# Layer 0 of a two-layer decoder trunk: every middle tile's second product pair by blocks, with weight sums made by transfers

## The chip, the cores and the metric

The kernel runs on one core of one Trainium2 chip. The metric is device time in microseconds (us) of one launch. A core has five engines that work side by side, each from its own queue in order: TensorE (PE; its weight loads are listed apart as PEld), VectorE (DVE), ScalarE (ACT), GpSimd (POOL) and SyncE (SP), which here issues transfers. Transfers run on 16 DMA engines. Engines wait for each other by semaphores.

## The reference

One inference step of a trunk of two layers over 576 tokens: 512 of a prompt and 64 of eight samples. All data is float32, the model width is 1024 and the width of each branch 2048. Layer 0 is a gated short convolution, layer 1 an mLSTM block with four heads. What concerns layer 0:

```python
def short_conv_mixer(h, buf, w_in, conv_w, w_out):
    b_gate, c_gate, xa, z = jnp.split(h @ w_in, 4, axis=-1)
    u = c_gate * xa
    conv, new_buf = causal_dwconv(u, buf, conv_w)
    y = b_gate * conv * jax.nn.silu(z)
    return y @ w_out, new_buf
```

Here `h` is the RMS-normalised input (576 x 1024) and `w_in` is 1024 x 8192. Layer 1 projects to 2 x 2048, convolves, makes queries, keys and values (2048 x 2048 each), runs the chunked recurrence with its states and projects back. Each layer adds its output to x; a last RMSNorm follows.

## The kernel before

**Precision.** Each float32 product is made as three matmuls in a rounded format: an operand is split into a high part (a cast on ScalarE) and a low part (a subtraction on VectorE), and hi x hi, hi x lo and lo x hi are added up in PSUM. `parts_of` and `split_weights` split weights (128 x 512 each), `split` splits activations (128 x 576).

**Layout.** Weights lie in HBM as chunks `wts[c]` of 128 x 8 x 128: 128 output columns for all 1024 inputs, 512 KB. Layer 0 has 16 width tiles f of 128 columns; tile f has the chunks 4f (c_gate), 4f+1 (xa), 4f+2 (z) and 4f+3 (b_gate). The first two are its first pair, the last two its second pair.

**Two ways to make a pair.** The plain way (`products`, line 234) runs 8 input blocks x 3 matmuls x 2 token halves (256 and 320 columns) for each chunk, 96 matmuls for a pair. The way by blocks (`block_pair`, line 332) takes the pair as a 2 x 2 block matrix: two chunks by even and odd input blocks (a11, a12 of chunk r1; a21, a22 of chunk r2), against activations cut into two input halves and two token halves of 288. A scheme with seven products in place of eight makes the four output blocks, 7 x 4 x 3 = 84 matmuls of 288 columns for the pair. It needs sums of weight blocks: s1 = a21 + a22, s2 = s1 + a11, later s2 + a12 and a21 + a11. `block_weights(c1, c2)` loads r1 and r2 on SP's queue and then calls `block_sums` for s1 and s2 on VectorE (lines 297 and 298); the other two are made in `block_pair` by `add_up` (line 337). The order of products is a11, s1, s2, a12, a21, s2 again, a22; the results wait in PSUM banks (`bx`, `by`, `bw`) and in two scratch tiles, `pu` (halves p and u, lines 350 and 359) and `m5` (line 347), and leave by lines 382 to 385. The activation sums (`fs`, from `first_blocks`) are made once at the start.

**Layer 0's loop** runs over f. In step f it loads the weights of f's own second pair (blocks if f is in `SECOND`, otherwise plain by `raw_weights`), runs the *first* pair of tile f+1 by blocks, loads the first pair of tile f+2 (`block_weights(4f+8, 4f+9)`), and runs the *second* pair of tile f. Between the products `run` takes pieces of gating and convolution of tile f from the list `work` (lines 492 to 603). `SECOND` holds 3, 5, 7, 9, 11, 13. Four buffers `wr` hold raw chunks, so the loads for a pair wait for the pair before the last. The scratch tiles of layer 0 (`ws` for s1 and s2, `pu`, `m5`, from tile 11 on also `cx`) share seven buffers (`X`).

**Order.** The program is written as a list of operations. A planner with its own model of durations orders them on each engine and places the waits; a wait at the head of an engine's queue holds everything behind it. `issue_after` and the list `work` give hints.

**Layer 1's places that the change touches.** The projection `acc = gemm(80 + f, ...)` leaves PSUM either by a ScalarE copy and a VectorE multiply with `rb` (lines 695 and 696) or by a VectorE multiply straight from PSUM; the latter for 3 < f < 14. `spread` (line 745) copies the 64 sample tokens of a key or value tile into a fourfold pattern `dup` or `kd`, two copies on POOL; `by_token` (lines 754, 756) transposes tile and pattern on TensorE and stores them. For the first key and query pair made, head 3 and tile 0, two empty steps are put into `work` ahead of `by_token`. That pair is made by `gemm_first`.

Of the kernel before, what the change touches and what calls it, by code (L numbers as in the profile page):

```python
# [12 lines left out]
ALU = mybir.AluOpType  # L13
# [3 lines left out]
P = 128  # L17
# [3 lines left out]
NW = W // P  # L21
# [34 lines left out]
LAG = 6  # L56
AHEAD = 2
FH = 2
SECOND = tuple(range(3, 14, 2))
FI = 1  # L60
EARLY = 3.45
NEARLY = 10
# [5 lines left out]
def trunk(tc, io):  # L68
    nc = tc.nc
    ctx = ExitStack()  # L70
    with ctx:
# [34 lines left out]
        layer0 = [False]  # L106
# [22 lines left out]
        def block(name="blk"):  # L129
            uid[0] += 1  # L130
            return accs[0][1].tile([P, 512], F32, name=f"{name}{uid[0]}", tag="blk", bufs=4)[:, 0:HT]
# [12 lines left out]
        load = nc.sync.dma_start  # L144
        store = nc.sync.dma_start
        store_act = nc.scalar.dma_start

        cols = const.tile([P, NCOL], F32, name="cols")
        cst = const.tile([P, NCST], F32, name="cst")
# [150 lines left out]

        def block_weights(c1, c2, six=False):

            groups, behind = [], []
            for i in range(1 + six):
                r1, r2 = weight_tile(), weight_tile()
                for r, c_ in ((r1, c1 + i), (r2, c2 + i)):
                    latest[0] = load(out=r, in_=io["wts"][c_]).ins
                groups.append(block_sums(r1, r2, (8, 4)[i]))
                behind = [r1, r2] if i else []
            ahead_of[c1, c2] = groups, behind  # L310

        def block_pair(c1, c2, fs, xs, out1, out2, add, mid=None, then=None, pops=0, groups=None,
                       behind=()):

            if groups is None:
                groups, behind = ahead_of.pop((c1, c2))
            a11, a12, a21, a22, s1, s2 = range(6)
            fs = [fs[0:4], fs[4:6]]  # L320
            o11, o12, o21, o22 = out1[:, 0:HT], out1[:, HT:NT], out2[:, 0:HT], out2[:, HT:NT]
            pu = X(name="pu")
            p, u = pu[:, 0:HT], pu[:, HT:NT]
            tt = nc.vector.tensor_tensor

            def product(bank_, block_, form, start):
                ws = [parts_of(g[block_]) for g in groups]
                for n, (w, g) in enumerate(zip(ws, fs)):
                    for j, forms_ in enumerate(g):
                        hi, lo = forms_[form]  # L330
                        for i, (a, x) in enumerate(((w[0], hi), (w[0], lo), (w[1], hi))):
                            nc.tensor.matmul(bank_, a[:, j, :], x, start=(start and n + j + i == 0),  # L332
                                             stop=(n == len(groups) - 1 and j == len(g) - 1 and i == 2), skip_group_check=True)

            def add_up(out, block_):
                for g in groups:
                    tt(g[out], g[out], g[block_], ALU.add)  # L337

            bx = block("p1")
            product(bx, a11, "b11", True)  # L340
            by = block("p6")
            nc.scalar.activation(by, bx, AF.Copy, scale=-1.0)  # L342
            run(pops)
            bw = block("p5")
            product(bw, s1, "t1", True)
            m5 = X(HT, name="m5")
            nc.scalar.copy(m5, bw)
            run(pops)
            product(by, s2, "t2", False)
            nc.scalar.copy(u, by)  # L350
            add_up(s2, a12)
            product(bx, a12, "b21", False)
            add_up(a21, a11)
            run(pops)
            if pops:
                drip()
            product(by, a21, "t3", False)
            if xs is None or add:
                nc.scalar.copy(p, by)
            else:  # L360
                bv = block("p7")
                nc.scalar.copy(bv, by)
            product(bw, s2, "b22", False)
            run(pops)
            product(by, a22, "t4", False)
            run(pops)
            mid = list(mid or ())
            for go in mid[0:2]:
                go()
            wx = [parts_of(r[:, 4:8, :]) for r in behind]  # L370
            if then:
                block_weights(*then)
            if add:
                tt(p, p, m5, ALU.subtract)
                tt(o22, o22, p, ALU.add)
                tt(o12, o12, u, ALU.subtract)
                tt(o12, o12, bw, ALU.add)
                tt(o11, o11, bx, ALU.add)
                tt(o21, o21, by, ALU.add)
                return  # L380
            if xs is None:
                tt(o22, p, m5, ALU.subtract)
                nc.scalar.copy(o11, bx)
                tt(o12, bw, u, ALU.subtract)
                nc.scalar.copy(o21, by)
                return
            plain(bx, bw, c1 + 1, xs, None, wx[0:1])
            nc.scalar.copy(o11, bx)
            if mid:
                nc.scalar.copy(o12, bw)  # L390
            tt(o12, o12 if mid else bw, u, ALU.subtract)
            for go in mid[2:3]:
                go()
            if pops:
                drip()
            plain(by, bv, c2 + 1, xs, None, wx[1:2])
            nc.scalar.copy(o21, by)
            if mid:
                nc.scalar.copy(o22, bv)
            tt(o22, o22 if mid else bv, m5, ALU.subtract)  # L400
            for go in mid[3:]:
                go()
# [278 lines left out]
        for f in range(NW):  # L681
            if f % 4 == 0:
                ext = T(352, name="ext")
                load(out=ext, in_=io["exb"][f // 4])
            ext_f = ext[:, 88 * (f % 4):88 * (f % 4) + 88].rearrange("p (b t) -> p b t", t=11)
            if f < 2:
                u = raws[f]
                nc.vector.tensor_tensor(u, u, rb, ALU.mult)
            else:
                acc = gemm(80 + f, 1, h2)  # L690
                u = T(name="xm")
                if 3 < f < NW - 2:
                    nc.vector.tensor_tensor(u, flat(acc), rb, ALU.mult)
                else:
                    nc.scalar.copy(u, flat(acc))
                    nc.vector.tensor_tensor(u, u, rb, ALU.mult)
            us.append(u)
            if f >= 8:
                xm.append(split(u))
            elif f % 2:  # L700
                fm.append(forms(us[f - 1], u))

            cv = []

            def begin(f=f, u=u, ext_f=ext_f, cv=cv):
                cv.append(T(name="xc"))
                cv.extend(conv_steps(cv[0], u, ext_f, [col(f"cb{j}", f) for j in range(4)]))
                cv[1]()

            def end(f=f, u=u, ext=ext, cv=cv):  # L710
                nc.gpsimd.tensor_copy(cpb[:, f, :], u[:, NP - 3:NP])
                nc.scalar.activation(cv[0], cv[0], AF.Silu, bias=col("cbias", f))
                store_act(out=xcs[f], in_=cv[0])
                if f % 4 == 3:
                    store(out=io["exb_out"][f // 4], in_=ext)
                if f == NW - 1:
                    store(out=io["cpb_out"], in_=cpb)

            slow.extend([begin] + [lambda s=s, cv=cv: cv[s]() for s in (2, 3, 4)] + [end])
            if f >= LAG:  # L720
                for _ in range(5):
                    drip()
            if f == NW - 3:
                block_weights(96, 98)
# [14 lines left out]
                else:  # L739
                    nc.vector.tensor_tensor(gacc[:, a:b], g[:, 0:b - a], gacc[:, a:b], ALU.add)  # L740

        def spread(t, dup):

            for u in range(2):
                nc.gpsimd.tensor_copy(
                    dup[:, 128 * u:128 * u + 128].rearrange("p (g s t) -> p g s t", g=4, s=4),
                    t[:, NP + 32 * u:NP + 32 * u + 32].rearrange("p (g t) -> p g t", t=8)
                    .unsqueeze(2).broadcast_to([P, 4, 4, 8]))
# [155 lines left out]
        for h in (3, 0, 1, 2):  # L904
            st = heads[h]
            for dt in range(4):
# [19 lines left out]
                if dt % 2 == 0:  # L926
                    st["kd"].append(T(512, name="kd"))
                dup = st["kd"][-1][:, 256 * (dt % 2):256 * (dt % 2) + 256]
                spread(k, dup)
                if (h, dt) == (3, 0):  # L930
                    work.extend([lambda: None] * 2)
                work.append(lambda k=k, dup=dup, h=h, dt=dt: by_token(
                    k, dup, KSCALE, kps[h][dt].rearrange("p (i d) -> p i d", d=128),
                    kss[h][:, :, 128 * dt:128 * dt + 128]))
# [670 lines left out]
def _chunks(w):  # L1605
    k, m = w.shape
    return w.reshape(k // D, KD, P, m // P, P).transpose(3, 0, 2, 1, 4)


def _arrays(a):  # L1610
# [5 lines left out]
    kq = np.stack([_chunks(f["b_w_k"][0]), _chunks(f["b_w_q"][0])], 1)  # L1616
    wts = np.concatenate([t.reshape(-1, P, KD, P) for t in (
        ain, _chunks(f["a_w_out"][0]), bin_[:NW], _chunks(f["b_w_v"][0]), kq, bin_[NW:], _chunks(f["b_w_out"][0]))], 0)
    cols = np.zeros((P, NCOL), np.float32)

    def put(name, v):
# [80 lines left out]
```

## Time and profile before

| | |
|---|---|
| median of 3 runs | 1684.31 us (1682.43 to 1685.41) |
| the profiled execution | 1682.5 us, span 1680.7 us, granted TensorE clock 0.99 |
| TensorE busy | 1648.2 us (98%) |
| VectorE busy | 1121.4 us (67%) |
| ScalarE busy | 781.2 us (46%) |
| GpSimd busy | 107.9 us (6%) |
| HBM read, written | 213.89 MB, 63.66 MB |

How to read the profile: times are counted from the start of the span. A row of a group names line, engine, operation, tiles (out<-in) and shape, then the count, the busy time and the mean of one instruction in ns, and the idle time of the engine just before such instructions with what ended it. Matmuls are pipelined, so the 0.3 us shown for one is its latency; the pace of TensorE is the time between starts. VectorE's instructions overlap a little too. In a view by windows each engine's column is its busy time within the window and, in brackets, the instructions that touch it; PEclk is the clock that was granted, 1.00 being full. A row of the timeline begins with start and duration; square brackets show the idle time before it and what ended it. In a list of waits a row ends with the total, the number of waits and the longest. A row of transfers gives the size and the median time from issue to landing.

### The profile page before, as it was taken

What the parts mean: (1) busy time and instruction counts of PE and PEld (TensorE: products, weight loads), DVE (VectorE), ACT (ScalarE), POOL (GpSimd) and SP (SyncE); (2) the same over time, 40 slices, a digit from 0 to 9 for tenths busy, and PEclk for the clock granted to TensorE, in tenths of its full rate; (3) what the DMA queues carried; (4) which work ended last, traced back from release to release, by engine and by line L of the source; (5) the groups of instructions that cost most, each with busy time, mean ns of one, the idle gap of its engine ahead of it and who ended that gap; (6) DMA issues with size and microseconds to landing.
All of it is one profiled execution on the core that took longest, in us unless ns stands there. A gap on an engine that the chain in (4) does not pass through costs nothing. (4 is left out here: it accounts for less than half of the span.)

```text
span 1680.7 us, 31096 instructions
## 1 busy us (share of the span) xinstructions
PE 1648.2 (98%) x12161; PEld 1569.9 (93%) x12161; DVE 1121.4 (67%) x2108; ACT 781.2 (46%) x1548; POOL 107.9 (6%) x241
## 2 busy tenths in 40 slices
PE   9999999999999999999899999999999998998998
PEld 9999999999999999999899989998988787988998
DVE  7988888874336975556856456456468567687775
ACT  5555555543224554535544334344345456555421
POOL 0000000000000000000211010101002000000000
PEclk9999999999999999999999999999999899999999
DMA  5233223333432434535434554453655687997982
GB/s 197 73 96 93 96 88 105 92 104 125 128 114 91 145 116 137 170 116 161 143 107 145 156 183 151 154 182 126 200 184 212 203 275 249 336 341 280 369 305 105
DMA packets 109794, 279.57 MB, mean 166 GB/s; under 512 B 11312, under 2 KB 33712, under 8 KB 109648
## 3 DMA queue, kind: packets, MB, share of 16 engines
q1 hardware_dynamic: 94288, 260.27, 47.2%
q10 hardware_dynamic: 15360, 17.32, 3.0%
q8 instruction: 95, 1.56, 0.4%
q14 instruction: 51, 0.42, 0.1%
HBM read 213.89 MB, written 63.66 MB: 165 GB/s over the span
## 5 line engine op out<-in xcount | busy, mean ns | idle before, releaser
L332 PE MATMUL p<-hi,wh 128*128 128x288 f32 x1316 | 389.3, 297 | 2.1 <-ACT p L342 1.5
L332 PE MATMUL p<-lo,wh 128*128 128x288 f32 x1316 | 387.6, 295 | 0.0
L332 PE MATMUL p<-hi,wl 128*128 128x288 f32 x1316 | 386.7, 295 | 0.0
L234 PE MATMUL acc<-hi,wh 128*128 128x256 f32 (+1 forms) x1328 | 288.9, 299 | 6.2 <-ACT num L1288 5.0
L234 PE MATMUL acc<-lo,wh 128*128 128x256 f32 (+1 forms) x1328 | 288.4, 297 | 0.0
L234 PE MATMUL acc<-hi,wl 128*128 128x256 f32 (+1 forms) x1328 | 287.1, 297 | 0.0
L332 PEld LDWEIGHTS p<-hi,wh 128*128 128x128 f32 x1316 | 247.3, 188 | 10.4 <-DVE ws L337 4.1
L263 ACT CAST wh<-wr 128x256 fp32r<-128x256 f32 (+1 forms) x266 | 152.0, 572 | 225.0 <-PE p L332 120.6
L332 PEld LDWEIGHTS p<-lo,wh 128*128 128x128 f32 x1316 | 247.7, 188 | 0.0
L332 PEld LDWEIGHTS p<-hi,wl 128*128 128x128 f32 x1316 | 247.0, 188 | 0.0
L214 ACT CAST wh<-wr 128x512 fp32r<-128x512 f32 x202 | 124.8, 620 | 239.3 <-PE acc L234 181.0
L234 PEld LDWEIGHTS acc<-hi,wh 128*128 128x128 f32 x1328 | 224.1, 190 | 11.7 <-ACT num L1288 5.2
L264 DVE TENSOR_TENSOR wl<-wr,wh 128x256 fp32r<-128x256 f32 (+1 forms) x266 | 163.1, 627 | 96.2 <-ACT wh L263 94.2
L234 PEld LDWEIGHTS acc<-hi,wl 128*128 128x128 f32 x1328 | 223.7, 190 | 1.5 <-issue 1.3
L234 PEld LDWEIGHTS acc<-lo,wh 128*128 128x128 f32 x1328 | 224.1, 190 | 0.5 <-issue 0.2
L215 DVE TENSOR_TENSOR wl<-wr,wh 128x512 fp32r<-128x512 f32 x202 | 138.7, 688 | 110.7 <-ACT wh L214 102.5
L263 ACT CAST wh<-ws 128x512 fp32r<-128x512 f32 (+1 forms) x177 | 99.9, 566 | 208.6 <-PE p L332 120.7
L264 DVE TENSOR_TENSOR wl<-ws,wh 128x512 fp32r<-128x512 f32 (+1 forms) x177 | 108.7, 620 | 57.6 <-ACT wh L263 57.5
L1222 DVE SCALAR_TENSOR_TENSOR c<-c,cols,r 128x512 f32<-128x512 f32 x128 | 91.3, 739 | 31.6 <-PE r L1221 26.2
L417 PE MATMUL p<-hi,wh 128*128 128x288 f32 x496 | 109.2, 300 | 0.0
L417 PE MATMUL p<-hi,wl 128*128 128x288 f32 x496 | 107.3, 295 | 0.0
L417 PE MATMUL p<-lo,wh 128*128 128x288 f32 x496 | 107.0, 295 | 0.0
(382 smaller groups left out, 2572.8 us busy)
## 6 DMA issues: line engine op xcount, KB each, us to landing
wr<-wts SPq DMA_DIRECT2D x222, 512.0 KB, 3.6
c<-cs SPq DMA_DIRECT2D x112, 512.0 KB, 5.9
cs_out<-c SPq DMA_DIRECT2D x64, 512.0 KB, 6.4
x<-xcs SPq DMA_DIRECT2D x20, 288.0 KB, 4.7
x<-xT SPq DMA_DIRECT2D x16, 288.0 KB, 4.2
xcs<-xc ACTq DMA_DIRECT2D x16, 288.0 KB, 2.5
ld<-xcs SPq DMA_DIRECT2D x16, 288.0 KB, 8.1
cp_out<-cp ACTq DMA_DIRECT2D x16, 257.0 KB, 7.0
```

Of the source, the lines that this page charges most:

```text
L214: last_act[0] = nc.scalar.copy(hi, raw[:, 4 * i:4 * i + 4, :]).ins
L215: nc.vector.tensor_tensor(lo, raw[:, 4 * i:4 * i + 4, :], hi.bitcast(F32), ALU.subtract)
L234: nc.tensor.matmul(acc[:, o:o + j - i], a[:, k % 4, :], x[:, i:j], start=(first and k == 0 and p == 0), stop=(last and k == 7 and p == 2))
L263: last_act[0] = nc.scalar.copy(hi, src).ins
L264: nc.vector.tensor_tensor(lo, src, hi.bitcast(F32), ALU.subtract)
L332: nc.tensor.matmul(bank_, a[:, j, :], x, start=(start and n + j + i == 0), stop=(n == len(groups) - 1 and j == len(g) - 1 and i == 2), ski ...
L417: nc.tensor.matmul(b, a[:, k % 4, :], x[:, t:t + HT], start=bool(start) and k == 0 and i == 0, stop=(k == n - 1 and i == 2), skip_group_ch ...
L1222: ins = nc.vector.scalar_tensor_tensor(ct[:, j, :], ct[:, j, :], dec[:, o + j:o + j + 1], r, ALU.mult, ALU.add).ins
```

## The change

In layer 0, `SECOND` now holds 2 to 14, so seven more second pairs (tiles 2, 4, 6, 8, 10, 12, 14) run by blocks. The chunks that run by blocks are stored with the even input blocks first, so that a11, a12, a21 and a22 are contiguous halves.

In layer 0 `block_weights` no longer sums on VectorE. It loads r1 and r2, loads a21 a second time into s1 (256 KB, on SP's queue), and issues two transfers on POOL's queue that read from HBM and add into SBUF: a22 into s1, and a11 into a21. s2 = s1 + a11 is made on VectorE in `block_pair`, when the pair begins; `add_up(s2, a12)` stays; `add_up(a21, a11)` is left out in layer 0. Layer 1 keeps its sums as they were.

In layer 1, tile 3 of the first projection leaves PSUM by the VectorE multiply, `spread` for head 3, tile 0 copies on ScalarE, and the two empty steps there go.

```diff
-SECOND = tuple(range(3, 14, 2))
+SECOND = tuple(range(2, 15))
...
+        add_load = nc.gpsimd.dma_start
...
         def block_weights(c1, c2, six=False):

+            if layer0[0]:
+
+                r1, r2 = weight_tile(), weight_tile()
+                for r, c_ in ((r1, c1), (r2, c2)):
+                    latest[0] = load(out=r, in_=io["wts"][c_]).ins
+                a11, a12, a21, a22 = [r[:, i:i + 4, :] for r in (r1, r2) for i in (0, 4)]
+                s1, s2 = [X(512, name="ws").rearrange("p (k x) -> p k x", x=P) for _ in range(2)]
+                load(out=s1, in_=io["wts"][c2][:, 0:4, :])
+                add_load(out=s1, in_=io["wts"][c2][:, 4:8, :], accum_op=ALU.add)
+                add_load(out=a21, in_=io["wts"][c1][:, 0:4, :], accum_op=ALU.add)
+                ahead_of[c1, c2] = [(a11, a12, a21, a22, s1, s2)], []
+                return
...
             bx = block("p1")
+            if layer0[0]:
+                tt(groups[0][s2], groups[0][s1], groups[0][a11], ALU.add)
             product(bx, a11, "b11", True)
...
-            add_up(a21, a11)
+            if not layer0[0]:
+                add_up(a21, a11)
...
-                if 3 < f < NW - 2:
+                if 2 < f < NW - 2:
                     nc.vector.tensor_tensor(u, flat(acc), rb, ALU.mult)
...
-        def spread(t, dup):
+        def spread(t, dup, copy=nc.gpsimd.tensor_copy):
...
-                nc.gpsimd.tensor_copy(
+                copy(
...
-                spread(k, dup)
-                if (h, dt) == (3, 0):
-                    work.extend([lambda: None] * 2)
+                spread(k, dup, *[nc.scalar.copy] * ((h, dt) == (3, 0)))
...
+    blk = [c for c in range(8, 64) if c % 4 < 2 or c // 4 in SECOND]
+    wts[blk] = wts[blk][:, :, [0, 2, 4, 6, 1, 3, 5, 7]]
```

## The prediction

> **What bounds the kernel now.** I read the page first, its busy shares and forty slices.
>
> ```profile
> PE 1648.2 (98%) x12161; PEld 1569.9 (93%) x12161; DVE 1121.4 (67%) x2108; ACT 781.2 (46%) x1548; POOL 107.9 (6%) x241
> PE   9999999999999999999899999999999998998998
> ```
>
> TensorE is the bound nearly everywhere. Two things can then shorten the run: fewer matmuls, or a pause of TensorE that goes. Layer 0 is in the first nine slices, so next I cut it with the view by windows, two width tiles (one plain second pair, one by blocks) to a window, and one stretch with block products alone, counting line 332.
>
> ```profile
> core 0: us, PE busy (x) PEld busy (x) DVE busy (x) ACT busy (x) POOL busy (x), PEclk, DMA share, GB/s
> 42.00:84.00 42.00, 41.34 (x311) 40.88 (x310) 39.40 (x71) 23.49 (x45) 0.96 (x3) 1.00 0.22 73
> ...
> 84.00:130.10 46.10, 46.10 (x350) 46.10 (x349) 37.85 (x65) 24.62 (x50) 1.17 (x2) 1.00 0.33 102
> ...
> 314.70:360.90 46.20, 46.20 (x350) 46.20 (x350) 39.05 (x68) 24.75 (x50) 1.17 (x2) 1.00 0.29 93
> sum 276.90, PE 276.90 PEld 276.90 DVE 234.31 ACT 148.13 POOL 7.03; mean PE 46.15 PEld 46.15 DVE 39.05 ACT 24.69 POOL 1.17
> ```
>
> ```profile
> 200.60:213.80 13.20, 13.20 (x102) 13.20 (x101) 1.00 0.26 81
> ```
>
> Look at three columns. PE is as long as its window, at clock 1.00: no pause between 84 and 361 us. The counts include two matmuls that reach in from before, so the block stretch holds 100 starts in 13.20 us, 0.132 us each, and two tiles hold 348 (three block pairs of 84 and one plain pair of 96). DVE is busy 39.05 of 46.15 us, 85%, so it is close behind.
>
> **The change, part by part.**
>
> *Seven more pairs by blocks (tiles 2, 4, ... 14).* A block pair is 84 matmuls of 288 columns, 84 x 0.132 = 11.09 us. A plain pair takes what the other 252 leave of the two-tile period: 46.15 - 252 x 0.132 = 12.89 us. Each conversion saves 1.80 us of TensorE, seven save 12.6 us, and all of it shows as long as TensorE stays gapless.
>
> *What VectorE and ScalarE pay.* Rows by shape, VectorE over 84 to 360 us, then ScalarE and the short VectorE form over 0 to 400 us:
>
> ```profile
> L264 DVE TENSOR_TENSOR wl<-wr,wh 128x512 fp32r<-128x512 f32 x72 | 49.4, 686 | 7.5 <-ACT wh L263 6.4
> L264 DVE TENSOR_TENSOR wl<-ws,wh 128x512 fp32r<-128x512 f32 x54 | 37.1, 687 | 12.4 <-ACT wh L263 12.4
> L297 DVE TENSOR_TENSOR ws<-wr 128x512 f32<-128x512 f32 x18 | 12.4, 689 | 7.7 <-DMA wr<-wts 7.7
> ```
>
> ```profile
> L263 ACT CAST wh<-wr 128x512 fp32r<-128x512 f32 x80 | 49.5, 619 | 63.3 <-PE p L332 40.8 <-PE acc L234 20.4 <-ACT pu L350 0.9
> ...
> L342 ACT ACTIVATE p<-p 128x288 f32<-128x288 f32 x20 | 7.9, 393 | 0.0
> ...
> L382 DVE TENSOR_TENSOR cx<-pu,m 128x288 f32<-128x288 f32 x14 | 6.3, 450 | 0.0
> ```
>
> And a stretch of VectorE's timeline, which serves the next part too:
>
> ```profile
> 196.84 0.68 DVE L264 TENSOR_TENSOR wl<-wr,wh 128x512 fp32r<-128x512 f32 x1
> ...
> 202.82 0.68 DVE L298 TENSOR_TENSOR ws<-ws,wr 128x512 f32<-128x512 f32 x1
> 203.42 0.68 DVE L337 TENSOR_TENSOR wr<-wr,wr 128x512 f32<-128x512 f32 x1
> ...
> 208.65 0.69 DVE L264 TENSOR_TENSOR wl<-wr,wh 128x512 fp32r<-128x512 f32 x1 [0.62 <-ACT wh L263]
> 210.25 0.69 DVE L264 TENSOR_TENSOR wl<-ws,wh 128x512 fp32r<-128x512 f32 x1 [0.90 <-ACT wh L263]
> ```
>
> A 512-wide VectorE operation lasts 0.69 us but frees the engine after 0.60 (starts 202.82 and 203.42). Per two tiles VectorE now makes 25 splits and 12 weight sums; afterwards 28 splits (four block pairs of 7) and 8 sums, since only two of the four sums of a pair stay: s2 = s1 + a11 at the pair's start, and the later s2 + a12. That is 37 against 36 long operations, and two more short ones (L382's form, 0.37 us freed). So 39.05 - 0.60 + 0.74 = 39.2 us in a period of 44.35 (336 x 0.132): 88%, more even than now, when the block tile alone carries 14 splits and 8 sums. ScalarE gains three casts of 0.62 and six copies of 0.39: 24.69 + 4.2 = 28.9 of 44.35. Both lie beside TensorE; I cost them at nothing, and the cover is the 12% of VectorE that stays idle. The new order inside the weight chunks costs nothing: the strided wr halves and the contiguous ws take 686 and 687 ns.
>
> *The sums made by transfers.* A pair now issues two loads of 512 KB on SP; it will issue a third there (s1, 256 KB), and two adding transfers of 256 KB on POOL's queue: s1 += a22, which waits for s1's load, and a21 += a11, which waits for r2's load. 27 pairs do so (14 first, 13 second): about 21 MB more. Behind the waits on POOL stand only the cpa copies of two columns, which nothing in the stage reads; behind SP's third issue (0.33 us) stand the next pair's loads and ext. What matters is whether s1 is whole in time. One chain shows the room: VectorE above, SP's second load for a pair, and ScalarE's first evacuation of that pair.
>
> ```profile
> 197.54 0.33 SPq L307 DMA_DIRECT2D wr<-wts  x1
> ```
>
> ```profile
> 213.28 0.39 ACT L342 ACTIVATE p<-p 128x288 f32<-128x288 f32 x1
> ```
>
> The split at 196.84 frees r2's buffer, the load goes at 197.54, and the pair that it feeds has its first split at 208.65, 11.1 us later. Its first product ends at 213.28, so TensorE started it at 213.28 - 12 x 0.132 = 211.7. The s2 sum stands at the head of VectorE's queue for this pair, with the a11 split behind it; TensorE is held when s1 lands later than 211.7 - 0.60 - 0.69 = 210.4, 12.9 us after the load's issue. Prices for transfers, from the DMA view over 84 to 420 us and, last, the page:
>
> ```profile
> wr<-wts SPq DMA_DIRECT2D x58, 512.0 KB, 3.5
> x<-xT SPq DMA_DIRECT2D x3, 288.0 KB, 4.0
> exa_out<-ext SPq DMA_DIRECT2D x4, 160.0 KB, 1.8
> ```
>
> ```profile
> ld<-xcs SPq DMA_DIRECT2D x16, 288.0 KB, 8.1
> ```
>
> No row shows an adding transfer or one issued by POOL. The nearest in size lie between 1.8 and 8.1 us; I take x<-xT's 4.0, nearest in both size and time, for s1's load and again for the adding. Then s1 is whole 0.33 + 4.0 + 4.0 = 8.3 us after r2's issue (3.9 to 16.5 between the ends): 4.6 us early, cost nothing. At 16.5 it is 3.6 us late in each of 27 pairs, 97 us; that end is a rival below. a21 follows s1 on the queue, and its split comes three products (4.8 us) later. s1's load must also find one of the seven X buffers free; five are held at that point (s1 and s2 of the pair that runs, pu and m5 of the one that ends, this s1), seven from tile 11 on, where cx joins them, so a few loads may go late by part of the 4.6 us: also nothing.
>
> In sentences apart: the Trainium skill, DMA: Bandwidth & Descriptors, "Anatomy of one DMA — SWDGE (gpsimd) path", fits 2.0 us + bytes / 436e3 for such transfers. As an estimate by that page 256 KB is 2.6 us and s1 would be whole 0.33 + 2.6 + 2.6 = 5.5 us after r2's issue; the sum would be the same.
>
> *First key and query pair of layer 1, head 3: the copies of k move from POOL to ScalarE, and two empty steps go.* POOL's timeline; line 745 by tile kd; VectorE; TensorE; windows:
>
> ```profile
> 829.42 7.50 POOL L745 COPY kd<-k 128x128 f32<-128x128 f32 x2 [23.19 <-issue]
> ```
>
> ```profile
> L745 POOL COPY kd<-k x4: 288/736/7263, 829.4 to 858.6; 128x128 f32<-128x128 f32 x4
> ```
>
> ```profile
> 834.05 0.45 DVE L287 TENSOR_TENSOR hl<-x,hl 128x288 fp32r<-128x288 f32 x1
> ...
> 836.46 0.44 DVE L379 TENSOR_TENSOR q<-q,p 128x288 f32<-128x288 f32 x1
> ```
>
> ```profile
> 833.37 0.29 PE L332 MATMUL p<-hl,wh 128*128 128x288 f32 x1
> 836.74 0.56 PE L756 MATMUL tb<-cst,kd 128*128 128x128 f32 x2 [3.08 <-POOL kd L745]
> 837.06 0.38 PE L332 MATMUL p<-hl,wh 128*128 128x288 f32 x1
> ...
> 842.91 0.30 PE L332 MATMUL p<-hi,wl 128*128 128x288 f32 x1
> ```
>
> ```profile
> 836.70:840.80 4.10, 4.06 (x19) 3.97 (x20) 1.28 (x3) 1.12 (x3) 1.75 (x7) 0.58 0.11 46
> ```
>
> One copy, 0.29 us at its shortest, takes 7.26, TensorE waits 3.08 us for it, and then runs at granted clock 0.58 until 840.8. Without the wait the next late thing is hl's low half, done at 834.50, so the matmul of 837.06 runs at about 834.55, and that of 842.91, 32 starts on, at 834.55 + 32 x 0.132 = 838.8: 4.1 us gained. ScalarE pays two copies; the nearest row is L342's 0.393 us for 288 columns, so at most 0.8 us for a queue that TensorE's splits share. I set 1.0 us against it, for the copies and for transposes issued two steps earlier before k is ready: 3.1 us net, with 0 and 4.1 as ends.
>
> The Trainium skill, SBUF — State Buffer, "Who interferes with whom", says that a VectorE instruction with two inputs in SBUF shuts out a GpSimd one that reads SBUF. The trace agrees: the copy ended 0.22 us after VectorE began 836.46, whose p is in PSUM. The same section lets GpSimd's writes pass, descriptors among them. By that the layer 0 issues are not held and the sum stands; were they held like this copy, 7.3 us more, s1 would come 8.3 + 7.3 - 12.9 = 2.7 us late per pair.
>
> *Tile 3 of layer 1's first projection: ScalarE's copy out of PSUM becomes VectorE's multiply.*
>
> ```profile
> 519.42 0.54 PE L234 MATMUL acc<-hi,wh 128*128 128x256 f32 x2 [1.04 <-ACT xm L695]
> ```
>
> ```profile
> 518.74 1.18 ACT L695 COPY xm<-acc 128x576 f32<-128x576 f32 x2
> ```
>
> The wait is for the first of the two copies (tile 2's, 0.65 us), and that one stays; the multiply was there before. I take 0; the ends are a gain of 1.04 if the first copy moves up and a loss as large if VectorE comes to the bank later.
>
> **Sum.** The profiled execution took 1682.5 us, span 1680.7. 12.6 + 3.1 = 15.7 us less: 1666.8, on the median of 1684.31 1668.6. This kernel's runs spread over 0.18%, so 0.2% (3.4 us) is about what a measurement can tell from no change.
>
> **Rivals.**
>
> 1. *The adding transfers land late* (slower). Place: VectorE's s2 sum at the head of each pair. For it: no row prices such a transfer, and the 8.1 us row gives 3.6 us late per pair. Against: layer 0 moves about 95 GB/s, that row comes from a busier stage. It decides when s1 is whole more than 12.9 + 15.7/27 = 13.5 us after r2's issue; at 16.5 the time is 1668.6 + 97 = 1766; just past the bound it is 1684 to 1700.
> 2. *VectorE becomes the bound.* Besides 39.2 us it waits for ScalarE's casts, in this view over 84 to 360 us (six windows):
>
> ```profile
> DVE wl L264 <- ACT wh L263: 18.8, 32, 1.1
> ```
>
>    That is 3.1 us per window: 42.3 of 44.35. If ScalarE's longer list doubles these waits, it is 45.4, 1.05 us over TensorE's period, and 7.4 of the 12.6 us go: 1676.0. Trebled, 48.5 us would undo the gain.
> 3. *The copies on ScalarE do not free TensorE at head 3's first pair*: another wait takes 3 us there; 1671.7.
> 4. *No change at all*: (1) and (2) eat the gain just so; 1681 to 1688.
> 5. *More than forecast*: the 0.7 us that TensorE lacks in 42 to 84 us, tile 3's 1.04 us and the whole 4.1: 1684.3 - 12.6 - 4.1 - 1.7 = 1665.9.
>
> **Chances.** Forecast, 1667 to 1671: 0.45. More, 1664 to 1667: 0.10. Copies in vain, about 1671.7: 0.12. VectorE the bound, 1672 to 1680.9: 0.15. No change: 0.05. Slower: 0.13. Faster is 0.45 + 0.10 + 0.12 + 0.15 = 0.82. The range 1664 to 1678 leaves out the slower, the unchanged and the end of the VectorE case, some 0.2.
>
> **What would show it.** Right: between 84 and 360 us TensorE is gapless at about 22.2 us per tile, sums on VectorE come two per pair, s2's sum has no idle time before it that an adding transfer ends, and line 756 has no 3 us wait after POOL. Wrong: waits of ws, wl or p for a DMA on POOL's queue, an adding transfer of more than 8.5 us, or matmul starts spread beyond 0.132 us in tiles 2 to 14.

## The result, and the profile after

The changed kernel takes 1665.49 us (median, 1661.51 to 1668.9), the kernel before, measured with it, 1684.09: a ratio of 0.9893, 95% interval 0.9878 to 0.9908, some 18 us. Measured again, beside the first experiments, it was 1666.28 against 1681.84, 0.9914 (0.9897 to 0.9931), 15.6 us. The forecast was 1668.6, 15.7 us less. The profiled execution, the slowest of the four, took 1668.9 us, span 1667.0.

The page of the changed kernel, its busy times and the transfers that the change adds (size, then the median time from issue to landing):

```profile
PE 1637.3 (98%) x12077; PEld 1557.8 (93%) x12077; DVE 1122.6 (67%) x2117; ACT 805.9 (48%) x1612; POOL 146.9 (9%) x293
...
ws<-wts SPq DMA_DIRECT2D x27, 256.0 KB, 4.2
ws<-wts POOLq DMA_DIRECT2D x27, 256.0 KB, 5.1
wr<-wts POOLq DMA_DIRECT2D x27, 256.0 KB, 4.1
```

TensorE issues 84 matmuls fewer (7 pairs x 12) and stays at 98%. VectorE's total has hardly moved: in two tiles it makes three splits more, and four of twelve weight sums have gone.

Layer 0 by windows, two width tiles to a window; the first row is the start of the layer:

```profile
core 0: us, PE busy (x) PEld busy (x) DVE busy (x) ACT busy (x) POOL busy (x), PEclk, DMA share, GB/s
42.00:84.00 42.00, 41.39 (x312) 41.12 (x312) 38.42 (x70) 23.09 (x44) 5.47 (x8) 1.00 0.45 116
84.00:128.40 44.40, 44.40 (x337) 44.40 (x337) 38.11 (x68) 28.15 (x59) 8.19 (x10) 1.00 0.72 180
...
172.80:217.20 44.40, 44.40 (x338) 44.40 (x337) 38.75 (x69) 28.14 (x59) 7.96 (x10) 1.00 0.70 174
...
306.00:350.40 44.40, 44.40 (x337) 44.40 (x337) 39.28 (x69) 28.01 (x59) 8.15 (x10) 1.00 0.68 166
```

A window of 44.40 us holds two tiles exactly, TensorE fills it at clock 1.00 and has 336 starts in it, where before it took 46.15. VectorE is busy 38.1 to 39.6 us of it, ScalarE 28, and the DMA engines' share has gone from about 0.3 to 0.7.

One chain of transfers, as in the prediction: SP's queue (187.00 is s1's load, 191.32 that of r2), GpSimd's (line 312 adds into s1, line 313 into a21), and VectorE's s2 sum (line 354), which needs s1.

```profile
187.00 0.42 SPq L311 DMA_DIRECT2D ws<-wts  x1
191.32 0.33 SPq L308 DMA_DIRECT2D wr<-wts  x1
```

```profile
192.73 0.88 POOL L312 DMA_DIRECT2D ws<-wts  x1 [7.43 <-DVE u L615]
...
195.37 0.87 POOL L313 DMA_DIRECT2D wr<-wts  x1 [1.10 <-ACT pu L375]
```

```profile
201.04 0.68 DVE L354 TENSOR_TENSOR ws<-ws,wr 128x512 f32<-128x512 f32 x1
...
203.03 0.69 DVE L265 TENSOR_TENSOR wl<-wr,wh 128x512 fp32r<-128x512 f32 x1 [0.62 <-ACT wh L264]
```

The adding transfer of line 312 landed at 197.61, so s1 was whole 6.3 us after r2's issue (191.32) and 3.4 us before the sum, which began with no idle time. The issue cost GpSimd 0.88 us. Tile `ws` over 84 to 350 us says it for all pairs; the columns after the colon are the durations in ns, minimum, median and maximum:

```profile
L354 DVE TENSOR_TENSOR ws<-ws,wr x23: 678/683/693, 89.3 to 336.8; 128x512 f32<-128x512 f32 x23
L312 POOL DMA_DIRECT2D ws<-wts x23: 862/865/1177, 94.5 to 336.7; - x23
...
  DMA ws<-wts: 65.9, 11
```

The 65.9 us are GpSimd's own waits for s1's load; over this stretch no line has VectorE waiting for a transfer. Ahead of it one s2 sum, at 23.17 us, waited 1.34 us for one, and TensorE did not wait.

Head 3's first pair of layer 1, ScalarE, then TensorE, then the window behind it:

```profile
820.63 0.49 ACT L761 COPY kd<-k 128x128 f32<-128x128 f32 x2
```

```profile
822.19 0.40 PE L345 MATMUL p<-hl,wh 128*128 128x288 f32 x1 [0.69 <-DVE hl L288]
```

```profile
822.20:826.00 3.80, 3.80 (x28) 3.80 (x29) 3.80 (x10) 1.33 (x3) 1.68 (x5) 1.00 0.63 207
```

Both copies together take ScalarE 0.49 us. TensorE's 3.08 us wait for GpSimd has gone, what is late next is hl's low half (0.69 us), and the clock stays at 1.00, where 0.58 was granted.

### The profile page after: what moved, and what is told of

It reads as the page before. It is cut to its first block, busy times and chain, and to the rows that moved or that the text cites. A ratio compares the mean times of both kernels' runs of the same rounds, so it can differ in the third digit from the quotient of the medians.

```text
span 1667.0 us, 31245 instructions
## 1 busy us (share of the span) xinstructions
PE 1637.3 (98%) x12077; PEld 1557.8 (93%) x12077; DVE 1122.6 (67%) x2117; ACT 805.9 (48%) x1612; POOL 146.9 (9%) x293
## 5 line engine op out<-in xcount | busy, mean ns | idle before, releaser
L345 PE MATMUL p<-hi,wh 128*128 128x288 f32 x1512 | 446.0, 297 | 1.9 <-ACT p L357 1.3
L345 PE MATMUL p<-lo,wh 128*128 128x288 f32 x1512 | 444.4, 295 | 0.0
L345 PE MATMUL p<-hi,wl 128*128 128x288 f32 x1512 | 442.7, 295 | 0.0
L264 ACT CAST wh<-wr 128x512 fp32r<-128x512 f32 (+1 forms) x294 | 169.0, 577 | 214.5 <-PE p L345 123.5
L265 DVE TENSOR_TENSOR wl<-wr,wh 128x512 fp32r<-128x512 f32 (+1 forms) x294 | 182.0, 633 | 94.9 <-ACT wh L264 92.9
L235 PE MATMUL acc<-hi,wh 128*128 128x256 f32 (+1 forms) x1104 | 239.7, 298 | 3.8 <-ACT num L1302 2.4
L235 PE MATMUL acc<-hi,wl 128*128 128x256 f32 (+1 forms) x1104 | 238.8, 297 | 0.0
L235 PE MATMUL acc<-lo,wh 128*128 128x256 f32 (+1 forms) x1104 | 238.5, 297 | 0.0
L264 ACT CAST wh<-ws 128x512 fp32r<-128x512 f32 x198 | 113.0, 572 | 201.0 <-PE p L345 130.3
L265 DVE TENSOR_TENSOR wl<-ws,wh 128x512 fp32r<-128x512 f32 x198 | 123.2, 628 | 68.5 <-ACT wh L264 67.9
L433 PE MATMUL p<-hi,wh 128*128 128x288 f32 x496 | 109.2, 300 | 0.0
L433 PE MATMUL p<-hi,wl 128*128 128x288 f32 x496 | 107.3, 295 | 0.0
L433 PE MATMUL p<-lo,wh 128*128 128x288 f32 x496 | 106.9, 295 | 0.0
```

What stands on the lines that cost most here:

```text
L235: nc.tensor.matmul(acc[:, o:o + j - i], a[:, k % 4, :], x[:, i:j], start=(first and k == 0 and p == 0), stop=(last and k == 7 and p == 2))
L264: last_act[0] = nc.scalar.copy(hi, src).ins
L265: nc.vector.tensor_tensor(lo, src, hi.bitcast(F32), ALU.subtract)
L433: nc.tensor.matmul(b, a[:, k % 4, :], x[:, t:t + HT], start=bool(start) and k == 0 and i == 0, stop=(k == n - 1 and i == 2), skip_group_ch ...
```

## The experiments

**Where the gain sits.** Two kernels, each with one part undone or replaced. The first has `SECOND = tuple(range(3, 14, 2))` again and keeps all else.

> The sums made by transfers and both edits of layer 1 as in the change, but blocks for the second pair in tiles 3, 5, ... 13 alone as before: 84 matmuls more. Theory A (the gain of layer 0 is the matmuls left out): 12.3 to 12.6 us slower than the changed kernel, 1677 to 1681, and TensorE gapless at 46.15 us per two tiles. Rival B (part of the gain comes from relieving VectorE): less than 9 us slower.

Measured 1681.07 against 1681.84, ratio 0.9997 (0.9985 to 1.0009): 14.8 us slower than the changed kernel run beside it, theory A. Matmul for matmul its layer 0 ends 13.5 us behind the first trace of the changed kernel, 12.8 behind the second. It was not gapless, though: over 84 to 361 us six s2 sums waited for transfers, and one of them held TensorE (VectorE, then TensorE):

```profile
348.91 0.69 DVE L354 TENSOR_TENSOR ws<-ws,wr 128x512 f32<-128x512 f32 x1 [3.60 <-DMA ws<-wts]
```

```profile
350.86 0.40 PE L345 MATMUL p<-hi,wl 128*128 128x288 f32 x1 [0.68 <-DVE wl L265]
```

That is rival 1 on a small scale. The transfers by themselves gain nothing; the gain in layer 0 is the matmuls left out. This kernel also has both edits of layer 1, and is no faster than the kernel before: in its trace it is 2.9 us ahead of that of before at 1000 us, and level with it at the end. The second kernel makes all four sums on VectorE again:

```diff
-                load(out=s1, in_=io["wts"][c2][:, 0:4, :])
-                add_load(out=s1, in_=io["wts"][c2][:, 4:8, :], accum_op=ALU.add)
-                add_load(out=a21, in_=io["wts"][c1][:, 0:4, :], accum_op=ALU.add)
+                nc.vector.tensor_tensor(s1, a21, a22, ALU.add)
+                nc.vector.tensor_tensor(s2, s1, a11, ALU.add)
...
-            if layer0[0]:
-                tt(groups[0][s2], groups[0][s1], groups[0][a11], ALU.add)
...
-            if not layer0[0]:
-                add_up(a21, a11)
+            add_up(a21, a11)
```

> Tiles 2 to 14 by blocks as in the change, but all four weight sums of layer 0 made on VectorE, no adding transfers. Theory A (the transfers are what keeps VectorE off the bound): VectorE 39.2 + 8 x 0.60 = 44.0 us busy in a period of 44.35, besides 3 to 5 us of waits for ScalarE's casts, so the two-tile period grows to 46 to 48 us and 1674 to 1684 us come out, pauses of TensorE in layer 0 that VectorE ends. Rival B (VectorE bears 99% as it bears 96% in the block tiles of before): the same time as the changed kernel within 2 us.

Measured 1666.35, ratio 0.9911 (0.9892 to 0.993), the same as the changed kernel: rival B. Its windows:

```profile
84.00:128.40 44.40, 44.40 (x338) 44.40 (x337) 43.23 (x77) 28.12 (x59) 1.06 (x3) 1.00 0.33 101
...
306.00:350.40 44.40, 44.40 (x337) 44.40 (x336) 42.88 (x77) 27.96 (x59) 0.77 (x2) 1.00 0.29 92
```

VectorE is busy 97% of the time and TensorE still has no pause. Its waits for ScalarE's casts over 84 to 350 us, in the changed kernel and then in this one (total, count, longest):

```profile
DVE wl L265 <- ACT wh L264: 31.8, 57, 1.0
```

```profile
DVE wl L265 <- ACT wh L264: 6.1, 22, 0.4
```

The busier VectorE is, the less it waits; that the casts are further ahead when it comes to them is the likely reason. So those waits are not a fixed price to be added to busy time. Moving the sums to the queues frees 4.3 us of VectorE per window, which buys nothing here: without the adding transfers the change takes the same time.

The changed kernel was run beside these:

> The changed kernel itself once more, on the chip of the three beside it. The traces of before and after put the gain at 12.3 us in layer 0 and 3.9 us at head 3's first pair, 16.2 us: theory A expects 1667 to 1669 against 1684. The first median lay 18.6 us under before; theory B holds that the last stage gains too, and expects 1664 to 1666.

**How much room the chain of transfers has.** s1's adding transfer is issued twice, or three times, in a row.

```diff
                 add_load(out=s1, in_=io["wts"][c2][:, 4:8, :], accum_op=ALU.add)
+                add_load(out=s1, in_=io["wts"][c2][:, 4:8, :], accum_op=ALU.add)
```

> In layer 0 the adding transfer of a22 into s1 is issued twice, the second behind the first (so s1 holds a22 twice). In the changed kernel s1 was whole 6.3 us after r2's issue, 3.4 us before the s2 sum; a second transfer adds about 4.9 us to landing plus 0.9 us of issue, 11.2 to 12.1 us after r2's issue. Theory A (the prediction's deadline of 12.9 us holds): the s2 sums wait for a transfer on VectorE, but TensorE stays gapless at 44.4 us per two tiles and the time is within 2 us of the changed kernel. Theory B (the real margin is the 3.4 us seen before the s2 sum): each of 27 pairs is held 1.5 to 2.4 us, 40 to 65 us slower.

> In layer 0 the adding transfer of a22 into s1 is issued three times in a chain (s1 holds a22 three times). By the same sum s1 is whole 17 to 18 us after r2's issue. Theory A (deadline 12.9 us): 4 to 5 us late in each of 27 pairs, 110 to 140 us slower than the changed kernel, with waits of the s2 sum for a DMA on VectorE. Theory B (the loads of the following pairs move up, or the order is planned anew around a late s1, so that lateness is hidden): under 30 us slower.

Two: 1732.8 us, ratio 1.0298 (1.0276 to 1.0321), some 66 us above the changed kernel, 2.5 per pair. Three, in one run: 1783.77, some 117 above, 4.3 per pair. With two, over 84 to 350 us, the waits and the window, then one pair on SP's queue (203.91 is s1's load, 208.39 that of r2), GpSimd's, VectorE and TensorE:

```profile
DVE ws L355 <- DMA ws<-wts: 55.8, 16, 5.9
...
PE p L346 <- DVE wl L265: 33.4, 14, 5.4
```

```profile
84.00:350.00 266.00, 232.03 (x1633) 228.72 (x1633) 189.26 (x336) 137.15 (x284) 58.22 (x70) 0.94 0.69 160
```

```profile
203.91 0.47 SPq L311 DMA_DIRECT2D ws<-wts  x1
208.39 6.23 SPq L308 DMA_DIRECT2D wr<-wts  x2
```

```profile
210.23 0.86 POOL L312 DMA_DIRECT2D ws<-wts  x1 [7.83 <-DMA ws<-wts]
212.54 0.89 POOL L314 DMA_DIRECT2D wr<-wts  x1 [1.45 <-DVE wl L265]
214.60 0.87 POOL L313 DMA_DIRECT2D ws<-wts  x1 [1.18 <-DMA ws<-wts]
```

```profile
221.00 0.69 DVE L355 TENSOR_TENSOR ws<-ws,wr 128x512 f32<-128x512 f32 x1 [3.24 <-DMA ws<-wts]
```

```profile
224.29 0.40 PE L346 MATMUL p<-hi,wl 128*128 128x288 f32 x1 [1.82 <-DVE wl L265]
```

That is rival 1's mechanism, shown: the s2 sum waits for the transfer, TensorE for the a11 split behind it, and TensorE is idle for 34 of 266 us at clock 0.94. Neither theory had its numbers whole. The expectation priced the second transfer at 5 to 6 us; here s1 went from issue (203.91) to whole (220.98) in 17.1 us against 10.6 in the changed kernel, 6.5 more. s1's load took 5.7 us (5.1 in the changed kernel), the first adding transfer 4.0 (4.9), and the second, issued once the first had landed, 6.4; why it took longer is not shown, but a21's adding transfer (line 314) was under way on the same queue. s1 was whole 12.6 us after r2's issue, inside the 12.9 us of theory A, and TensorE was held 1.8 us in this pair all the same. In the next pair the sum waited 2.67 us and TensorE not at all; in the one after, s1 was whole 13.6 us after r2's issue and TensorE was held 4.4. So the deadline is not one number: in these three pairs it lay at 10.8, above 12.2 and at 9.2 us after r2's issue. A sum could begin 1.4 us late in the first and the third, and at least 2.7 in the second; with the 3.4 us seen in the trace of the changed kernel that makes a room of some 4.8 to 6.1 us.

**What the edit at head 3's first pair is worth.** First by itself, on the kernel before:

```diff
-                spread(k, dup)
-                if (h, dt) == (3, 0):
-                    work.extend([lambda: None] * 2)
+                spread(k, dup, *[nc.scalar.copy] * ((h, dt) == (3, 0)))
```

> The kernel before with one edit only: at head 3's first pair the copies of k on ScalarE and no empty steps. Theory A (the prediction's step: 4.1 us gained at the pair, of which 3.1 stay): 1682 - 3.1 = 1679 us, ratio 0.998. Theory B (the last stage gives most of it back, as in the changed kernel with the copies on GpSimd, which ended only 0.7 us later): 0.5 to 1 us, ratio 0.9995. By both the matmuls behind the pair start 3.8 to 4.1 us earlier at 838 us.

Measured 1678.42 against 1683.04, ratio 0.9977 (0.9966 to 0.9989), 3.9 us, theory A. Its TensorE at the pair:

```profile
834.58 0.40 PE L332 MATMUL p<-hl,wh 128*128 128x288 f32 x1 [0.66 <-DVE hl L287]
```

That is 0.03 us from the start that the prediction worked out for this matmul, 834.55. Then the other way round, the changed kernel with those three lines as before, measured twice:

> The changed kernel with the copies of k for head 3's first pair back on POOL and the two empty steps back. Theory A (the port: POOL's copy is shut out while VectorE runs with two inputs in SBUF, TensorE waits 3 us and then runs at clock 0.58): 3.5 to 4.2 us slower than the changed kernel, the POOL copy again 5 to 8 us long. Rival B (the long copy of before was an accident of its place in time): under 1 us slower, POOL copy under 1.5 us.

> A second measurement of the changed kernel with the copies of k at head 3's first pair back on GpSimd and the two empty steps back. The changed kernel stood at 0.9893 and 0.9914 of the kernel before. Theory A (the lag of 4 us at the pair reaches the end): 0.9922 to 0.9935, 1669.5 to 1671 us. Theory B (0.7 us of it does, as measured first, 0.9921 with an interval of 0.0022): 0.991, 1666.5 to 1668 us.

Measured 1667.02, ratio 0.9921 (0.9899 to 0.9943), and 1667.48, ratio 0.9901 (0.9886 to 0.9916): 0.7 us above the changed kernel that ran beside the first. The mean of the two ratios is 0.9911, that of the changed kernel's two 0.9904: 1.2 us, well under 4. Yet the wait is back (GpSimd, VectorE, TensorE, first run):

```profile
818.62 7.49 POOL L761 COPY kd<-k 128x128 f32<-128x128 f32 x2 [24.06 <-issue]
```

```profile
825.65 0.46 DVE L395 TENSOR_TENSOR q<-q,p 128x288 f32<-128x288 f32 x1
```

```profile
822.56 0.29 PE L345 MATMUL p<-hl,wh 128*128 128x288 f32 x1
825.94 0.56 PE L772 MATMUL tb<-cst,kd 128*128 128x128 f32 x2 [3.09 <-POOL kd L761]
826.26 0.38 PE L345 MATMUL p<-hl,wh 128*128 128x288 f32 x1
```

The window behind the wait, first run, then second:

```profile
825.90:829.90 4.00, 3.96 (x29) 3.87 (x30) 2.23 (x5) 1.32 (x3) 1.76 (x7) 1.00 0.12 47
```

```profile
825.10:829.20 4.10, 4.06 (x20) 4.01 (x20) 1.23 (x3) 0.99 (x3) 1.55 (x7) 0.58 0.09 38
```

The waits are alike, 3.09 and 3.08 us, but the clock behind them is not: it stayed at 1.00 in the first run, and fell to 0.58 in the second as in the kernel before. From one matmul on hl to the next the first run takes 3.70 us and the changed kernel 1.22 (820.97 to 822.19), so the wait alone costs 2.5 us; the slow clock, where it came, added 1.4 or 1.5. The prediction's 4.1 us counted it as certain.

Matmul for matmul both runs are 4 to 5 us behind the first trace of the changed kernel at 826 us, of which 1.6 and 0.8 were there ahead of the wait, still 2 to 4 behind up to 1390, and level or ahead at 1538. To see whether that last stage absorbs any delay, 90 extra products, with a result that nothing uses, were put at the same place:

```diff
+                if (h, dt) == (3, 0):
+                    def burn(x=fc[0]["t1"][0]):
+                        b = bank("burn")
+                        for _ in range(90):
+                            nc.tensor.matmul(b[:, 0:HT], x[:, 0:P], x, start=True, stop=True)
+                    work.append(burn)
```

> The changed kernel with 90 extra products of 128 x 288 (result unused) on TensorE at head 3's first key pair, 90 x 0.132 = 11.9 us. Theory A (what TensorE loses or gains there reaches the end whole, as the prediction's 3.1 us assumed): 1666.3 + 11.9 = 1678.2 us. Theory B (the stage between 1390 and 1540 us, where the DMA engines are full, gives back about 3 us of any shift made before it, as with the copies on GpSimd, which came 4 us late at 826 us and 0.7 us late at the end): the lag is about 12 us after the burn until 1390 us, and 8 to 9 us at the end, 1674.5 to 1675.5 us.

Measured 1677.27, ratio 0.9968 (0.9956 to 0.9979): 11.0 us by the medians, of 11.9 put in. That is nearer to theory A, 1678.2; theory B, 1674.5 to 1675.5, is unlikely, but the interval (1674.8 to 1678.6 us) does not quite shut it out. In its trace the lag is 10.1 us at the end against the first trace of the changed kernel and 11.5 against the second. What is left is that the pair's edit brought 3.9 us alone, and on top of the layer 0 part about 1 with an uncertainty of about 2. The difference goes between 1300 and 1550 us, and its cause is not settled. In that stretch even the two traces of the changed kernel move 3.5 us against each other: the second is 2.1 us behind at 1300 and 1.4 ahead at 1550. The time of one kernel also goes with its granted clock: of the 17 executions of the kernel before that ran beside the first experiments, the fastest, 1676.45 us, had 0.993 and the slowest, 1686.2, had 0.987. A difference of 1 to 3 us is hard to place against that.

**What held GpSimd's copy.** Memsets in place of the two copies; in the second of these kernels one also writes over k itself, so that it must run where the copy ran.

```diff
-                spread(k, dup, *[nc.scalar.copy] * ((h, dt) == (3, 0)))
+                if (h, dt) == (3, 0):
+                    nc.gpsimd.memset(k[:, NP:NP + 64], 0.0)
+                    for u in range(2):
+                        nc.gpsimd.memset(dup[:, 128 * u:128 * u + 128], 0.0)
+                    work.extend([lambda: None] * 2)
+                else:
+                    spread(k, dup)
```

> At head 3's first pair GpSimd writes zeros in place of the two copies of the samples' keys (the pattern is left out of the result), and the two empty steps are back. A memset writes and reads nothing. Theory A (the copy of 7.3 us was long because its reads of SBUF are held while VectorE runs operations with two SBUF inputs): a memset in the same place takes under 1 us, and TensorE's wait of 3.1 us for GpSimd is gone, as with the copies on ScalarE. Theory B (GpSimd as a whole is slow or held at this point, whatever it does): the memsets take about 7 us for the two and TensorE waits 3 us as before. Time: within 1 us of the changed kernel by A, 0 to 4 us above it by B.

> At head 3's first pair GpSimd writes zeros over the samples' columns of k itself, behind VectorE's write of k, and over the pattern (both are left out of the result), with the empty steps back. In the first such run the memsets waited for nothing and ran 12 us early, at 806 us; here the one on k must run where the slow copy ran, at about 818 us. Theory A (only GpSimd's reads of SBUF are held by VectorE's operations with two SBUF inputs): this memset takes 0.2 to 0.6 us there and TensorE does not wait 3 us for GpSimd. Theory B (GpSimd is held whatever it does): 3 to 7 us, and the transposes of k wait for it.

The first took 1667.55 us (ratio 0.9909, 0.9896 to 0.9923), but its memsets ran at 806 us, under other work, so it said nothing on the hold. The second, in one run of 1663.94 us, GpSimd and VectorE:

```profile
817.81 0.15 POOL L946 MEMSET k<- 128x64 f32 x1 [22.06 <-DVE k L393]
817.98 0.35 POOL L948 MEMSET kd<- 128x128 f32 x2
```

```profile
817.52 0.69 DVE L265 TENSOR_TENSOR wl<-ws,wh 128x512 fp32r<-128x512 f32 x1
818.12 0.45 DVE L274 TENSOR_TENSOR fb<-x,fa 128x288 f32<-128x288 f32 x1
```

Writing took 0.15 us in the same place in which one copy took 7.26, while VectorE ran the same kind of operations with two inputs; TensorE waited 0.67 us, for hl. That is theory A, in one run: what was held is GpSimd's copy, which reads SBUF, and not its writing. The end of the hold fits too: 7.26 us after its start the copy was done 0.22 to 0.23 us after VectorE began its first operation with an input in PSUM (`p` at 836.46 in the kernel before, at 825.65 above).

By the Trainium skill, SBUF — State Buffer, "Who interferes with whom", GpSimd's writes pass while its reads are shut out; these rows agree, and so do the issues of line 312, 0.86 us each next to a VectorE that is 88% busy.

**Two tiles more.** `SECOND = tuple(range(1, 16))`, with the chunks of tiles 1 and 15 reordered as well.

> The changed kernel with tiles 1 and 15 by blocks too (24 matmuls fewer). Theory A (a block pair saves 1.80 us wherever TensorE is gapless): 3.6 us less, 1662.5 us, ratio about 0.9885. Theory B (at the two ends of the layer the weights are not there in time: the first s2 sum already began 0.02 us after its transfer landed at 23.15 us, and tile 15 is followed by the projection): TensorE waits for the loads of tile 1 or 15 and the gain is 0 to 1.8 us, 1664.5 to 1666.3 us, or a loss at tile 1.

Measured 1673.15, ratio 0.9941 (0.9928 to 0.9953): some 7 us slower than the changed kernel, beyond either theory. TensorE, ScalarE and windows at tile 1:

```profile
68.67 0.61 PE L345 MATMUL p<-hi,wh 128*128 128x288 f32 x1 [5.86 <-ACT cx L401]
```

```profile
65.39 0.67 ACT L166 CAST hi<-cv 128x576 fp32r<-128x576 f32 x1 [2.06 <-DVE cv L663]
67.56 0.78 ACT L508 ACTIVATE cv<-u,cols 128x576 f32<-128x576 f32 x1 [1.50 <-DVE u L615]
68.24 0.38 ACT L401 COPY cx<-p 128x288 f32<-128x288 f32 x1
```

```profile
62.00:70.00 8.00, 2.14 (x12) 1.91 (x11) 7.23 (x15) 2.95 (x6) 1.93 (x3) 0.69 0.45 131
70.00:74.00 4.00, 4.00 (x25) 4.00 (x25) 2.91 (x6) 1.39 (x3) 0.00 (x0) 0.76 0.41 70
74.00:78.00 4.00, 4.00 (x32) 4.00 (x31) 2.08 (x3) 1.69 (x4) 0.00 (x0) 1.00 0.43 131
```

Not the loads: TensorE waits 5.86 us for ScalarE's copies out of PSUM, which stand behind two gating steps that wait for VectorE, and then runs at clock 0.76. TensorE also lacks about 1 us more than in the changed kernel at 350 to 372 and again at 800 to 822 us. What tile 15 does by itself was not run.

## Why the prediction was right, point by point

*Layer 0, 12.6 us.* Right. The period came out at 44.40 against 44.35, the layer ends 12.3 us earlier, and undoing the tiles alone takes it back (14.8 us). VectorE at 38.8 (39.2 forecast) and ScalarE at 28.1 (28.9) are as worked out.

*Cover of 12% on VectorE.* The cover was larger than needed. At 3% idle TensorE still did not wait. Rival 2 added the waits for casts to the busy time (42.3 of 44.35) and let them grow with ScalarE's load; they did grow, from 18.8 us in 276 to 31.8 in 266, but shrank to 6.1 when VectorE had more to do. That rival's addition was the wrong way to read a wait of an engine that has slack.

*The chain of transfers.* The outcome was right, its terms off both ways. Taken were 4.0 us for s1's load and 4.0 for the adding; in the chain shown they were 5.1 (187.00 to 192.06) and 4.9, with 0.7 between them, 10.6 from s1's issue. s1's load, however, was issued 4.3 us ahead of r2's, not behind it, so s1 was whole 6.3 us after r2's issue, not 8.3. The deadline of 12.9 was too generous by 2.1 and 3.7 us in two of the three pairs looked at with two adding transfers. The two errors went against each other: some 4.8 to 6.1 us of room where 4.6 were forecast, which is luck as far as the size goes. The issues on GpSimd were not held, at 0.86 us.

In a sentence apart: by the Trainium skill, DMA: Bandwidth & Descriptors, "Anatomy of one DMA — SWDGE (gpsimd) path", the estimate for 256 KB was 2.6 us; the page of this profile has 5.1 and 4.1 from issue to landing for the adding transfers, so the fit does not carry to them here. The prediction used the same figure for s1's load, which goes on SP's queue, not GpSimd's; that load took 4.2.

*Head 3's first pair, 3.1 us net.* The wait and the next late thing were right, the start to 0.03 us; alone the edit gave 3.9 (1.9 to 5.7). Of the 4.1 us, 2.5 are the wait and the rest the slow clock, which did not come each time. In the changed kernel 2.5 to 4 us stand at 826 us, but only a part that is hard to tell from nothing stands at the end. The deduction of 1.0 for ScalarE was too much, 0.49 us being all that the two copies took. The step that doesn't hold is that the two parts add up: without the pair's edit the change is worth 14.8 and 15.6 us where 12.6 was forecast, the pair alone 3.9, both together 15.6 to 18. That the total came out at the 15.7 forecast is so in part luck: 12.3 us are seen in layer 0, and in the traces without the pair's edit 2 to 4 more come behind 1300 us, where the prediction put nothing.

*Tile 3 of layer 1's projection, 0.* Right: the gap of 1.35 us there is the same in both traces.

## What to carry to other kernels

Where TensorE ran without a pause, as here between 84 and 350 us, a matmul left out was worth its issue interval, and the prices of side work mattered only where their cover ended: find that edge by doubling the suspect, not by its busy share. Try the plain form too: the adding transfers were built to relieve VectorE, and the sums left on VectorE took the same time. A wait of an engine that has slack is not a cost to add to its busy time; here it shrank from 31.8 to 6.1 us as the engine filled. A tile at the start of a loop isn't like the middle ones: at tile 1 the copies out of PSUM stood in ScalarE's queue behind work that waited.

## What the runs showed of the hardware that was not expected

- An adding transfer of 256 KB out of HBM took 4.1 to 5.1 us to land, about as long as a plain load of the size (4.2), and 0.86 us of GpSimd to issue. A second one chained on the same tile landed in 6.4 us and made the chain 6.5 us longer in the pair shown.
- A GpSimd copy of 128 x 128 took 7.26 us in each of three traces, through a row of some fifteen VectorE operations, most with two SBUF inputs, while a memset there (128 x 64) took 0.15 us: the hold lasted over the whole row, not for one operation.
- VectorE ran at 97% busy over 266 us without holding up TensorE.
- Behind the same wait of TensorE, 3.08 or 3.09 us, the granted clock was 0.58 over some 4 us in two traces (the kernel before, and the second with the copies back on GpSimd) and 1.00 in a third (the first with them back).
